# Attention's probabilities times values: from query-pair by key-pair groups to single key tiles, with the logits one to two steps ahead

## The chip, the core and the metric

The kernel runs on one core of a Trainium2 chip. The core has five engines with an instruction queue each: TensorE (PE in the profile; the loading of its weights is listed apart as PEld), VectorE (DVE), ScalarE (ACT), GpSimd (POOL) and SyncE (SP), which here only issues transfers. The engines meet through semaphores. Data lies in SBUF (128 partitions); TensorE writes to PSUM, which has eight banks of 128 x 512 float32. Sixteen DMA engines move data between HBM and SBUF.

The metric is the device time of one execution in microseconds (us), the median of several. A profiled execution gives one trace, whose span is a little shorter than that execution's own time.

## What is computed

A decoder block on one sequence of 1024 tokens and 1024 features, all in float32:

```python
xn   = rmsnorm(h, norm_mix_g);  proj = xn @ w_in
q, k, v = proj[:, :512], proj[:, 512:1024], proj[:, 1024:1536]      # 8 heads of 64
log_f = log_sigmoid(proj[:, 2560:] + b_forget);  c = cumsum(log_f)
logits = q @ k.T / 8 + c[:, None] - c[None, :], causal              # per head
att  = softmax(logits) @ v
u, vg = gelu(proj[:, 1536:2560]) in two halves                      # 8 groups of 64
sg   = u * (tril(w_spatial) @ rmsnorm(vg) per chunk of 128 + b_spatial)
h    = h + concat(att, sg) @ w_out
h    = h + (silu(g) * a) @ w_down,  a, g = causal conv3(rmsnorm(h) @ w_up)
out  = rmsnorm(h, norm_final_g)
```

TensorE takes a rounded float32 (fp32r) at full speed, so each operand is kept as a rounded high part and a low remainder, and a product is three matmuls: high x high, high x low, low x high.

## The kernel before

The whole program is one unrolled stream. The large products (`w_in`, `w_up`, `w_down`) are done by a seven-product block scheme, with sums and differences of blocks on VectorE and GpSimd. The stages in order of time: gate and value projections (from 0 us), queries and keys (from 106 us), spatial gating and the first head's logits (from about 180 us), the eight heads of attention (229 to 370 us), the output projection and second norm (from 370 us), the up products with the convolution (to 842 us), and the down products with the last norm (842 to 1058 us).

The order of an engine's instructions is set by the tile framework's scheduler from the order in which the program writes them, but for edges written by hand: `seq` chains every matmul and transpose of attention on TensorE in program order, `after` puts one instruction behind another on an engine, and while `act.on` and `dve.on` are set ScalarE and VectorE keep program order too (as they do in the first stage). A tile is a slot of a ring with a name; a new tile waits until the old one's last reader is done.

**One head of attention, before.** The queries are eight tiles of 128 rows (j = 0 to 7), the keys eight tiles of 128 (k). `logits_mm(h, j)` computes query tile j against the keys 0 to j with two matmuls for each 512 columns (L906, L907) into an "L" tile of two PSUM banks; there are two such tiles. `logits_min` (L919, VectorE) adds the causal mask, stores the row into `places[h, j//2]` in SBUF and takes the row's minimum (the logits carry a minus sign); `logits_exp` (L929, ScalarE) turns it into probabilities in place and sums the rows. `turn_p` (L935) transposes up to four 128 x 128 blocks of probabilities into one bank (L946, TensorE), ScalarE rounds them to the high part (L947), VectorE forms the low part (L948); the pair lies in a "pt" tile, of which there are three. `values` (L953) multiplies by the values: the stationary operand is V of one key tile, high and low part side by side (128 columns), the moving one the transposed probabilities.

A group was a pair of query tiles i (j = 2i and 2i + 1) by a pair of key tiles k0, k0 + 1: ten groups a head, in the order i = 3, 2, 1, 0. A matmul of a group covers one key tile and 256 query columns (128 on the diagonal). The result of four query tiles is gathered in one bank, `po`, and read by ScalarE and VectorE (L973, L974) when its last group is done.

The loop runs over 40 steps, five a head, two groups a step. In step n it issues the transposes of step n + 1, then the values of step n, and behind each group of values the logits of the next head that the table `NEXT` names: tile 7 in step 0, 6 in step 1, 5 and 4 in step 2, 3 and 2 in step 3, 1 and 0 in step 4. The exponentials of these run one step later, behind the step's casts (`last`, `due`; at the end of head 6 two batches are held back by a step). `fill` issues pieces of an independent product at the end of a step (`sg_out`: 12 matmuls of 512 columns each, the gating half of the output projection); `FILLS` names the steps: 0, 2 and 4 of head 0, and 1 and 4 of heads 1 to 5. Pieces, transposed groups and `po` share the other four banks. Heads 6 and 7 have no piece left, head 7 has no next head.

**The first tile, the gate's norm, the end.** The first stage loads x and weights in turns (L222, L223), scales x by its gain into high and low (`own`: ScalarE, then VectorE), splits the weights (`tsplit`: ScalarE high, VectorE low) and multiplies (`tmul`). `gate_norm` (L459) scales the gate's values with four wide VectorE multiplications (L466). The last stage ends with `finish` for the token tiles 4 to 7 (L1589): a square root, a reciprocal, one half of the row on ScalarE (tile 6: on VectorE, L1603), the other on VectorE (L1599), and one transfer to the output (L1604).

## Time and profile before

| what | value |
|---|---|
| median of 3 runs | 1058.76 us (1058.74 to 1059.16) |
| the profiled execution's own time, its span | 1059.72 us, 1058.0 us |
| TensorE busy | 1046.3 us (99%) |
| VectorE, ScalarE, GpSimd busy | 884.0 us (84%), 571.1 us (54%), 235.8 us (22%) |
| TensorE clock granted, mean | 0.999 |
| moved by DMA | 155.78 MB, 147 GB/s |

A row of a group view reads: line, engine, operation, output <- inputs, shapes, xcount, then busy time and mean duration of one, then the idle time of the engine before these instructions and what ended it. A row of the timeline reads: start in us, duration (of a merged run: from its start to its end), engine, line, operation, xcount, and in brackets the wait before it and what ended that. Durations of matmuls hold their latency, so that neighbours overlap: the time that one costs in a stream is the distance from start to start.

### The profile page before, as it was taken

Reading aid. Unit: us, or ns where it says so; the run is one execution under the profiler, and the core shown is the slowest. Engines: PE = TensorE matmul, PEld = TensorE weight load, DVE = VectorE, ACT = ScalarE, POOL = GpSimd, SP = SyncE. Lnnn points to the kernel's source line nnn. Section 1 sums busy time; section 2 is a strip of 40 time slices with the busy share of each in tenths; the row PEclk is TensorE's granted clock in tenths of the full one; section 3 lists DMA queues with packets and bytes.
Section 4 is the critical chain, followed back from the end, with each engine's and each line's share of the span. In section 5 each row is a group of like instructions: output and inputs, shape, how many; then the busy total and the mean of one; then the engine's idle time right before and its main releaser. Section 6 shows DMA issues by size and latency. Waiting matters only on the chain.

```text
span 1058.0 us, 14612 instructions
## 1 busy us (share of the span) xinstructions
PE 1046.3 (99%) x5156; PEld 880.3 (83%) x5156; DVE 884.0 (84%) x1297; ACT 571.1 (54%) x1013; POOL 235.8 (22%) x177
## 2 busy tenths in 40 slices
PE   9999999999999999999999999999999999999997
PEld 6988888988889888888888888888888888888885
DVE  6999787777778869998999989989897866897774
ACT  6776544456766746654444444444444544454653
POOL 0003241420420740154333323323321000000000
PEclk9999999999999999999999999999999999999999
DMA  9623466856555344222255322331322899333432
GB/s 323 219 8 134 129 162 167 224 153 190 168 163 170 122 174 173 72 89 100 80 170 179 120 96 94 120 122 59 132 96 80 302 328 314 102 99 100 146 119 94
DMA packets 67184, 155.78 MB, mean 147 GB/s; under 512 B 9028, under 2 KB 9748, under 8 KB 67112
## 3 DMA queue, kind: packets, MB, share of 16 engines
q1 hardware_dynamic: 65800, 154.82, 45.8%
q8 instruction: 40, 0.66, 0.3%
q14 instruction: 32, 0.26, 0.1%
q10 hardware_dynamic: 1312, 0.04, 0.1%
HBM read 111.96 MB, written 42.87 MB: 146 GB/s over the span
## 4 chain that ended last, share of the span: by engine, by line
PE 94%; DVE 2%; DMA 1%; ACT 1%; POOL 1%; issue 0%; SPq 0%; POOLq 0%; ACTq 0%; DVEq 0%
PE k L1529 20%; PE qc L1271 11%; PE qa L1271 11%; PE qd L1271 11%; PE ps L259 5%; PE qb L1271 5%; PE pb L259 5%; PE pb L965 3%; PE pb L946 3%; PE qa L417 2%; PE qc L417 2%; PE qd L417 2%; PE pl L906 2%; PE pl L907 2%; PE pf L990 1%; PE pf L992 1%
## 5 line engine op out<-in xcount | busy, mean ns | idle before, releaser
L1529 PE MATMUL k<-whb,wha 128*128 128x512 f32 x924 | 209.7, 389 | 0.0
L1529 PEld LDWEIGHTS k<-whb,wha 128*128 128x128 f32 x924 | 173.4, 188 | 36.2 <-DVE wha L161 0.2
L1271 PE MATMUL qc<-xT,whb 128*128 128x512 f32 x540 | 129.8, 389 | 0.2 <-ACT whb L155 0.2
L1271 PE MATMUL qa<-xB,wha 128*128 128x512 f32 x528 | 127.5, 390 | 0.0
L1271 PEld LDWEIGHTS qc<-xT,whb 128*128 128x128 f32 x540 | 101.3, 188 | 21.5 <-ACT whb L155 0.5
L1271 PEld LDWEIGHTS qa<-xB,wha 128*128 128x128 f32 x528 | 98.8, 188 | 20.9 <-DVE wha L161 0.4
L155 ACT CAST wha<-sg 128x512 fp32r<-128x512 f32 x77 | 47.8, 622 | 96.7 <-PE k L1529 86.4
L155 ACT CAST whb<-sg 128x512 fp32r<-128x512 f32 x82 | 50.5, 618 | 88.0 <-PE qc L1271 67.7
L161 DVE TENSOR_TENSOR wha<-sg,wha 128x512 fp32r<-128x512 f32 x77 | 52.7, 687 | 40.5 <-ACT wha L155 40.4
L947 ACT CAST pt<-pb 128x512 fp32r<-128x512 f32 (+1 forms) x80 | 42.2, 544 | 43.1 <-PE pb L946 34.2
L1271 PE MATMUL qd<-xB,whb 128*128 128x512 f32 x264 | 63.7, 389 | 0.0
L1271 PE MATMUL qd<-xT,whb 128*128 128x512 f32 x264 | 63.7, 389 | 0.0
L1155 POOL TENSOR_TENSOR sg<-raw 128x512 f32<-128x512 f32 x20 | 31.1, 1556 | 139.5 <-DVE whb L161 78.0
L1271 PE MATMUL qb<-xT,whb 128*128 128x512 f32 x252 | 61.0, 389 | 0.0
L161 DVE TENSOR_TENSOR whb<-sg,whb 128x512 fp32r<-128x512 f32 x82 | 57.0, 697 | 4.4 <-ACT whb L155 4.3
L948 DVE TENSOR_TENSOR pt<-pb,pt 128x512 fp32r<-128x512 f32 (+1 forms) x80 | 48.8, 634 | 12.3 <-ACT pt L947 11.0
L1271 PEld LDWEIGHTS qd<-xT,whb 128*128 128x128 f32 x264 | 49.5, 188 | 10.5 <-DVE u L1378 0.3
L1271 PEld LDWEIGHTS qd<-xB,whb 128*128 128x128 f32 x264 | 49.6, 188 | 10.3
L1271 PEld LDWEIGHTS qb<-xT,whb 128*128 128x128 f32 x252 | 47.2, 188 | 10.0 <-DVE whb L161 0.3
L965 PE MATMUL pb<-pt,V 128*128 128x256 f32 x320 | 52.1, 287 | 0.3 <-DVE pt L948 0.2
L1158 POOL TENSOR_TENSOR sg<-sg,raw 128x512 f32<-128x512 f32 x20 | 33.0, 1650 | 63.8 <-DVE whb L161 63.8
L965 PEld LDWEIGHTS pb<-pt,V 128*128 128x128 f32 x320 | 43.8, 190 | 2.6 <-DVE pt L948 0.4
(411 smaller groups left out, 2271.8 us busy)
## 6 DMA issues: line engine op xcount, KB each, us to landing
raw<-wup SPq DMA_DIRECT2D x44, 512.0 KB
sg<-hx SPq DMA_DIRECT2D x77, 256.0 KB
hx<-hs SPq DMA_DIRECT2D x44, 256.0 KB
hx<-ca SPq DMA_DIRECT2D x35, 256.0 KB
xT<-wdn SPq DMA_DIRECT2D x28, 256.0 KB
x<-kd SPq DMA_DIRECT2D x24, 256.0 KB
A<-xtok SPq DMA_DIRECT2D x8, 512.0 KB
raw<-wqk SPq DMA_DIRECT2D x8, 512.0 KB
```

Of the source, the lines that this page charges most:

```text
L155: act.copy(h, src)
L161: return eng.tensor_tensor(out=l, in0=src, in1=f32(h), op=ALU.subtract)
L259: pe.matmul(banks[m], xs(n, xi, k)[:, ms], w[:, wi, :], start=(first and k == 0 and c == 0 and (own or m % 2 == 0)), stop=(k == 3 and c == ...
L417: pe.matmul(ps, w[:, wi, ks], xs(n, xi, k), start=(first and c == 0), stop=(c == 11), skip_group_check=True)
L946: seq(pe.transpose(ptr[:, c:c + P], tj[jj][:, k * P:(k + 1) * P], ident))
L947: casts.append(act.copy(pt[:, 0, 0:w], ptr[:, 0:w]))
L948: los.append(dve.tensor_tensor(out=pt[:, 1, 0:w], in0=ptr[:, 0:w], in1=f32(pt[:, 0, 0:w]), op=ALU.subtract))
L965: seq(pe.matmul(po[0][:, oo:oo + n], lhs, pt[:, s, o:o + n], start=(k == 0 and s == 0), stop=(s == 1 and half)))
L1155: pool.tensor_tensor(out=s[0], in0=a21, in1=a22, op=ALU.add)
L1158: pool.tensor_tensor(out=s[3], in0=s[1], in1=a12, op=ALU.add)
L1271: pe.matmul(ps, w[:, wi, ks], xb[:, xi, k, :], start=(first and n == 0), stop=(n == 11), skip_group_check=True)
L1529: pe.matmul(banks[bk + m], xh[:, xi, ms], wh[:, wi, :], start=(first and p_ == 0 and n == 0), stop=(p_ == NP - 1 and n == 2), skip_group_c ...
```

## The change

Attention. A group is now a single key tile by up to four query tiles: nine groups a head, each exactly one bank of four blocks (`GROUPS`; small ones share a bank). `(1, k)` are the query tiles 4 to 7 against key tile k, `(0, k)` the tiles 0 to 3; `spans` lists the parts of a group with their columns. `turn_p` rounds all 512 columns. `values` does two matmuls a part (high and low of the probabilities), of 512, 384, 256 or 128 columns; `po` becomes two banks, one for each half of the queries, opened by `(1, 0)` and `(0, 2)` and read after `(1, 6)` and `(0, 3)`. The steps stay five a head, the last with one group. The next head's logits come two tiles a step in steps 0 to 3 and none in step 4. The piece of step 1 moves to step 2 in heads 1 to 5. The order edge on the reciprocal moves from the minimum of tile 6 to that of tile 5.

First stage. The first x tile is loaded in two halves around the first weights, scaled in halves, and the first weights' high part is made by VectorE. Gate. The four multiplications of `gate_norm` come behind the low part of the last values' weights (`gates["high"]`). End. Token tile 6 goes out in two halves.

```diff
--- before.py
+++ after.py
@@ -18,7 +18,7 @@
 NFF = 22
 WARM = 11
 
-FILLS = {(-1, j): 1 for j in (5, 3, 2)} | {(h, s): 1 for h in range(6) for s in ((0, 2, 4) if h == 0 else (1, 4))}
+FILLS = {(-1, j): 1 for j in (5, 3, 2)} | {(h, s): 1 for h in range(6) for s in ((0, 2, 4) if h == 0 else (2, 4))}
 FCFG = ("b", 4, 4)
 
 
@@ -218,7 +218,10 @@
     tmp = [[sb("pt", [P, 2, 512]) for _ in range(3)], [sb("t01", [P, 2, 512]), tj[:, 0], tj[:, 1]]]
     ua = [sb("raw", [P, 2, 512]) for _ in range(4)]
     gb = []
-    for k in range(4):
+    sp.dma_start(out=xr("x11", 0)[:, 0:256], in_=xT[0:P, 0:256])
+    sp.dma_start(out=ua[0][:, 0, :], in_=wuv[0, :, 0, :])
+    sp.dma_start(out=xr("x11", 0)[:, 256:512], in_=xT[0:P, 256:512])
+    for k in range(1, 4):
         load_x("x11", k, k, 0)
         sp.dma_start(out=ua[k][:, 0, :], in_=wuv[k, :, 0, :])
     sp.dma_start(out=cp, in_=cpk)
@@ -243,9 +246,12 @@
     vgt = [sb("G", [P, 4, 512]) for _ in range(2)]
     ut = [sb("A", [P, 4, 512]) for _ in range(2)]
 
+    newest = []
+
     def tsplit(src, gate=None, n=512, tag=None):
         w = sb(tag, [P, 2, n], F32R) if tag else ring(n=n)
         d = split_w(src, (w[:, 0], w[:, 1]))
+        newest[:] = [d]
         if gate:
             behind(d, gate)
         return w
@@ -269,9 +275,16 @@
     B = [bank() for _ in range(4)]
     S = [sbank() for _ in range(4)]
     act.on = dve.on = True
-    for k in range(4):
+    w = ring()
+    split_w(ua[0][:, 0, :], (w[:, 0], w[:, 1]), "dve")
+    for o in (slice(0, 256), slice(256, 512)):
+        h, l, src = xs("B11", 0, 0)[:, o], xs("B11", 1, 0)[:, o], xr("x11", 0)[:, o]
+        act.activation(h, src, AF.Copy, scale=gk(0))
+        dve.scalar_tensor_tensor(out=l, in0=src, scalar=gk(0), in1=f32(h), op0=ALU.mult, op1=ALU.subtract)
+    tmul(B, w, "B11", 0, True, apart=True)
+    for k in range(1, 4):
         own("B11", xr("x11", k), k, k)
-        tmul(B, tsplit(ua[k][:, 0, :]), "B11", k, True, apart=(k == 0))
+        tmul(B, tsplit(ua[k][:, 0, :]), "B11", k, True)
     for k in range(4):
         own("B21", xr("x21", k), k, 4 + k)
         tmul(S, tsplit(ua[k][:, 1, :]), "B21", k, True)
@@ -463,7 +476,7 @@
             for t in (0, 2):
                 v3 = vgt[hf][:, t:t + 2, :].rearrange("p t (g d) -> p (t g) d", d=64)
                 r = gms[:, hf * 32 + t * 8:hf * 32 + t * 8 + 16]
-                dve.tensor_tensor(out=v3, in0=v3, in1=r.unsqueeze(2).to_broadcast((P, 16, 64)), op=ALU.mult)
+                behind(dve.tensor_tensor(out=v3, in0=v3, in1=r.unsqueeze(2).to_broadcast((P, 16, 64)), op=ALU.mult), "high")
 
     gate_part(1, 0)
     gate_part(1, 2)
@@ -484,6 +497,7 @@
     W[0].sums()
     W[0].last_sum()
     values_high(3)
+    gates["high"] = newest[0]
     keep(S, 1)
     for m in range(4):
         dve.tensor_tensor(out=ut[1][:, m, :], in0=B[m], in1=ut[1][:, m, :], op=ALU.subtract)
@@ -918,7 +932,7 @@
         mn = sml.tile([P, 1], F32, tag="mn", name=nm("mn"))
         m = dve.tensor_tensor_reduce(out=places[h, i][jj], in0=ps[:, 0:n], in1=msk[:, 1024 - n:1024], scale=1.0,
                                      scalar=lim[:, 0:1], op0=ALU.add, op1=ALU.min, accum_out=mn)
-        if h and j == 6:
+        if h and j == 5:
             after(tc, m, recips[h - 1])
         if h and j == 3:
             after(tc, m, los[-1])
@@ -932,48 +946,52 @@
     def logits(h, j):
         logits_exp(h, j, logits_min(h, j, logits_mm(h, j, place())))
 
+    GROUPS = [((1, k),) for k in range(5)] + [((1, 5), (1, 7)), ((1, 6), (0, 2)), ((0, 0),), ((0, 1), (0, 3))]
+
+    def spans(g):
+
+        h, parts = g
+        c = 0
+        for half, k in parts:
+            j = max(k, 4 * half)
+            w = (4 * half + 4 - j) * P
+            yield half, k, j, c, w
+            c += w
+
     def turn_p(g):
 
-        h, i, k0 = g
-        tj = places[h, i]
         ptr = bank()
         pt = sb("pt", [P, 2, 512], F32R)
-        diag = k0 == 2 * i
-        blocks = [(k0, 0, 0), (k0, 1, 128)] + ([(k0 + 1, 1, 256)] if diag else
-                                              [(k0 + 1, 0, 256), (k0 + 1, 1, 384)])
-        w = 384 if diag else 512
-        for k, jj, c in blocks:
-            seq(pe.transpose(ptr[:, c:c + P], tj[jj][:, k * P:(k + 1) * P], ident))
-        casts.append(act.copy(pt[:, 0, 0:w], ptr[:, 0:w]))
-        los.append(dve.tensor_tensor(out=pt[:, 1, 0:w], in0=ptr[:, 0:w], in1=f32(pt[:, 0, 0:w]), op=ALU.subtract))
+        for half, k, j0, c, w in spans(g):
+            for j in range(j0, 4 * half + 4):
+                o = c + (j - j0) * P
+                seq(pe.transpose(ptr[:, o:o + P], places[g[0], j // 2][j % 2][:, k * P:(k + 1) * P], ident))
+        casts.append(act.copy(pt[:, 0, :], ptr))
+        los.append(dve.tensor_tensor(out=pt[:, 1, :], in0=ptr, in1=f32(pt[:, 0, :]), op=ALU.subtract))
         return pt
 
-    po = [None]
+    po = [None, None]
 
     def values(g, pt):
-        h, i, k0 = g
-        if i % 2 == 1 and k0 == 0:
-            po[0] = bank()
-        oc = (i % 2) * 256
-        for s in range(2):
-            for k in (k0, k0 + 1):
+        h, x = g[0], None
+        for half, k, j, c, w in spans(g):
+            new = (half, k) in ((1, 0), (0, 2))
+            if new:
+                po[half] = bank()
+            o = (j - 4 * half) * P
+            for s in range(2):
                 lhs = V[k // 2][:, k % 2, h, :, :].rearrange("p s d -> p (s d)")
-                half = k == 2 * i + 1
-                o = (k - k0) * 256
-                n = 128 if half else 256
-                oo = oc + (128 if half else 0)
-                seq(pe.matmul(po[0][:, oo:oo + n], lhs, pt[:, s, o:o + n], start=(k == 0 and s == 0),
-                              stop=(s == 1 and half)))
-        if i % 2 == 0 and k0 == 2 * i:
-            p, hh = h // 2, h % 2
-            o = slice((i // 2) * 512, (i // 2) * 512 + 512)
-            r = slice(hh * 64, hh * 64 + 64)
-            if attF[p] is None:
-                attF[p] = sb("H", [P, 2, 1024])
-            x = act.copy(attF[p][r, 0, o], po[0][64:128, :])
-            dve.tensor_tensor(out=attF[p][r, 0, o], in0=po[0][0:64, :], in1=attF[p][r, 0, o], op=ALU.add)
-            return x
-        return None
+                seq(pe.matmul(po[half][:, o:o + w], lhs, pt[:, s, c:c + w], start=(new and s == 0),
+                              stop=(s == 1 and (half, k) in ((1, 6), (0, 3))), skip_group_check=True))
+            if (half, k) in ((1, 6), (0, 3)):
+                p, hh = h // 2, h % 2
+                q = slice(half * 512, half * 512 + 512)
+                r = slice(hh * 64, hh * 64 + 64)
+                if attF[p] is None:
+                    attF[p] = sb("H", [P, 2, 1024])
+                x = act.copy(attF[p][r, 0, q], po[half][64:128, :])
+                dve.tensor_tensor(out=attF[p][r, 0, q], in0=po[half][0:64, :], in1=attF[p][r, 0, q], op=ALU.add)
+        return x
 
     def sg_out(whs):
         for hf in range(2):
@@ -1015,10 +1033,9 @@
                 pool.tensor_tensor(out=w[hf][:, 1], in0=src, in1=f32(w[hf][:, 0]), op=ALU.subtract)
             wo.append(w)
 
-    STEPS = [[(h, i, 2 * c) for i in (3, 2, 1, 0) for c in range(i + 1)] for h in range(8)]
-    STEPS = [s[n:n + 2] for s in STEPS for n in range(0, 10, 2)]
-
-    NEXT = (((7,), ()), ((6,), ()), ((5,), (4,)), ((3,), (2,)), ((1,), (0,)))
+    STEPS = [[(h, g) for g in GROUPS[n:n + 2]] for h in range(8) for n in range(0, 9, 2)]
+
+    NEXT = (((7,), (6,)), ((5,), (4,)), ((3,), (2,)), ((1,), (0,)), ((),))
 
     def fill(key):
         for _ in range(FILL.get(key, 0)):
@@ -1598,10 +1615,13 @@
             act.activation(y[tt][:, done], y[tt][:, done], AF.Copy, scale=r)
         dve.scalar_tensor_tensor(out=y[tt][:, todo], in0=y[tt][:, todo], scalar=r, in1=gfb[:, todo],
                                  op0=ALU.mult, op1=ALU.mult)
+        rows_ = out[tt * P:(tt + 1) * P, :]
         if tt == 6:
-
+            sp.dma_start(out=rows_[:, todo], in_=y[tt][:, todo])
             dve.tensor_scalar(out=y[tt][:, done], in0=y[tt][:, done], scalar1=r, scalar2=None, op0=ALU.mult)
-        sp.dma_start(out=out[tt * P:(tt + 1) * P, :], in_=y[tt])
+            sp.dma_start(out=rows_[:, done], in_=y[tt][:, done])
+        else:
+            sp.dma_start(out=rows_, in_=y[tt])
 
     def gain(tt, half):
         dve.tensor_tensor(out=y[tt][:, half], in0=y[tt][:, half], in1=gfb[:, half], op=ALU.mult)
```

## The prediction

> **What bounds the kernel now.** I read the page first, then the table by stage, then attention grouped by shape, then timelines of TensorE, VectorE and ScalarE inside one head, at the start and at the end.
>
> ```profile
> span 1058.0 us, 14612 instructions
> PE 1046.3 (99%) x5156; PEld 880.3 (83%) x5156; DVE 884.0 (84%) x1297; ACT 571.1 (54%) x1013; POOL 235.8 (22%) x177
> PE 94%; DVE 2%; DMA 1%; ACT 1%; POOL 1%; issue 0%; SPq 0%; POOLq 0%; ACTq 0%; DVEq 0%
> ...
> 229.40:347.00 117.60, 117.22 (x773) 105.07 (x772) 91.58 (x193) 79.73 (x180) 20.73 (x20) 1.00 0.58 171
> 347.00:371.00 24.00, 23.14 (x176) 21.09 (x174) 19.78 (x41) 19.01 (x45) 17.68 (x19) 1.00 0.42 139
> 371.00:1040.00 669.00, 668.83 (x2977) 552.52 (x2977) 577.94 (x752) 326.35 (x519) 144.78 (x88) 1.00 0.41 137
> ```
>
> The columns of the stage rows are stretch, length, then busy time and count of PE, PEld, DVE, ACT, POOL, then granted clock, DMA share, GB/s. TensorE is the bound nearly everywhere, at full clock. In attention's first six heads (to 347) it is busy 117.22 of 117.60 us while VectorE has 26 us and ScalarE 38 us to spare. In the last two heads, without filler, it loses some 0.9 us and the other two come within 4 to 5 us of it. After 371 it never rests until the tail, so what attention saves arrives at the end undiminished. The question is what the values' matmuls cost TensorE, and whether the new order leaves it waiting.
>
> **Part 1, the values' matmuls.** Their price is the distance from start to start.
>
> ```profile
> 836.08 2.72 PE qc L1271 x12
> ...
> 262.28 0.28 PE L906 MATMUL pl<-x 128*128 128x256 f32 x1
> 262.40 0.29 PE L907 MATMUL pl<-x,x 66*128 66x256 f32 x1
> 262.52 0.64 PE L965 MATMUL pb<-pt,V 128*128 128x256 f32 x4
> 263.00 0.40 PE L906 MATMUL pl<-x 128*128 128x512 f32 x1
> ...
> 265.72 0.34 PE L906 MATMUL pl<-x 128*128 128x384 f32 x1
> 265.89 0.34 PE L907 MATMUL pl<-x,x 66*128 66x384 f32 x1
> 266.07 1.04 PE L946 MATMUL pb<-ident,t 128*128 128x128 f32 x8
> 266.86 0.65 PE L965 MATMUL pb<-pt,V 128*128 128x256 f32 x4
> ...
> 268.45 0.28 PE L907 MATMUL pl<-x,x 66*128 66x128 f32 x1
> 268.56 0.45 PE L990 MATMUL pf<-whl,G 128*128 128x512 f32 x1
> ```
>
> 512 columns cost 2.72 / 12 = 0.227 us. 256 cost 0.12 (262.28 to 262.40 to 262.52, and four from 262.52 to 263.00). 384 cost 0.17 to 0.18; I take 0.175. 128 cost 0.11, hardly less than 256: so narrow a matmul pays for something other than its columns.
>
> ```profile
> L965 PE MATMUL pb<-pt,V 128*128 128x256 f32 x256 | 50.3, 304 | 0.3 <-DVE pt L948 0.2
> L965 PE MATMUL pb<-pt,V 128*128 128x128 f32 x64 | 14.3, 223 | 0.0
> L948 DVE TENSOR_TENSOR pt<-pb,pt 128x512 fp32r<-128x512 f32 x48 | 32.1, 687 | 9.6 <-ACT pt L947 9.2
> L948 DVE TENSOR_TENSOR pt<-pb,pt 128x384 fp32r<-128x384 f32 x32 | 17.2, 554 | 2.7 <-ACT pt L947 1.7
> L947 ACT CAST pt<-pb 128x512 fp32r<-128x512 f32 x48 | 27.2, 586 | 18.7 <-PE pb L946 14.2 <-PE pb L965 4.3
> L947 ACT CAST pt<-pb 128x384 fp32r<-128x384 f32 x32 | 15.3, 479 | 24.3 <-PE pb L946 20.0 <-PE pb L965 3.4 <-ACT t L869 0.9
> ```
>
> A head now has 256 / 8 = 32 matmuls of 256 columns and 8 of 128: 32 x 0.12 + 8 x 0.11 = 4.72 us. From the diff's spans a head gets 12 of 512 (key tiles 0 to 4 of the upper half, tile 0 of the lower), 4 of 384, 4 of 256 and 4 of 128: 12 x 0.227 + 4 x 0.175 + 4 x 0.12 + 4 x 0.11 = 4.34 us. The columns are the same (9216); 16 matmuls are gone, half of the 128-wide ones among them. Saved: 0.376 us a head, **3.01 us in eight heads**. The blocks transposed stay 36 a head. All of this lies on TensorE's path.
>
> The Trainium skill's TensorE page (TensorE: Matmul & The Clock Gate, Back-to-back issue gap) puts a warm matmul at N / 2.4 + 2.5 ns, that is 216, 109 and 56 ns for 512, 256 and 128 columns. By it a head would go from 3.94 to 3.90 us, and all heads together would save 0.3 us. The rows disagree (227, 120 and 110 ns) and go into the sum.
>
> Casts and low parts go from ten to nine a head, all 512 wide: VectorE 72 x 0.687 = 49.5 for 48 x 0.687 + 32 x 0.554 = 50.7 us, ScalarE 72 x 0.586 = 42.2 for 43.5. Behind TensorE this costs and brings nothing; in heads 6 and 7, where less covers them, at most 0.3 us.
>
> **Part 2, the order: logits two tiles a step, piece moved, edge moved.** Work on TensorE is unchanged; what may change is waiting.
>
> ```profile
> L919 DVE CUSTOM_DVE_ANT_0 H<-pl,t,lim x16: 876/1074/1286, 233.8 to 356.1; 128x1024 f32<-128x1024 f32 x4, 128x896 f32<-128x896 f32 x4, 128x768 f32<-128x768 f32 x4, 128x640 f32<-128x640 f32 x4
> ```
>
> Steps 0 and 1 now hold the four long minima, 4 x 1.074 = 4.3 us, beside four low parts (2.7): 7.0 us of VectorE. TensorE has there eight values matmuls (1.8), the logits of tiles 7 to 4 (4 and 2 + 2, then 2 + 2 and 2 + 2 matmuls: 0.91 + 0.80 + 0.69 + 0.67 = 3.1) and sixteen transposes (1.6, from 266.07 to 266.86 for eight): 6.5 us. So VectorE falls behind by about half a microsecond, unless durations overlap. Who would wait: logits tile 5 needs tile 7's "L" tile, free when its minimum is done. Laid out from a head's start, TensorE does transposes, values, logits 7, values, logits 6 (0.8 + 0.45 + 0.91 + 0.45 + 0.80 = 3.4), then transposes and values again, and wants that tile at 4.7; VectorE ends its two low parts at about 2.8 (cast 0.59 and low part 0.69 behind the transposes, the second behind a free "pt" tile) and the minimum 1.28 later, at 4.1. Carried on in the same way, with the next two low parts ahead of the next minima, tiles 4, 3 and 2 have margins of about 0.6, 0.3 and 0.4. Then step 2 brings the piece, 12 x 0.227 = 2.7 us without much for VectorE, in heads 1 to 5, and that is where it catches up. The exponentials of tiles 7 and 6 come in step 1 instead of steps 1 and 2; they are needed at step 4's transposes as before. The edge on the reciprocal has behind it only VectorE's low parts, and the rows it needs are summed a step earlier than now. Taken: 0. The bound of a gain: TensorE's waits in head 7, where late exponentials sit between ScalarE's casts, could go, because the next head's logits are now done a step sooner:
>
> ```profile
> 361.24 0.52 PE L946 MATMUL pb<-ident,H 128*128 128x128 f32 x3 [0.29 <-DVE pt L948]
> 365.62 0.66 PE L946 MATMUL pb<-ident,wy 128*128 128x128 f32 x4 [0.49 <-DVE pt L948]
> 362.96 0.73 ACT L929 ACTIVATE wy<-wy,mn 128x512 f32<-128x512 f32 x1
> ```
>
> From start to start TensorE loses more there than the brackets say: four transposes at 360.32 should end in 0.4 us and the next come at 361.24; three at 364.63 take until 365.62 where 0.3 would do; together 1.2 us. The bound of a loss: the last two heads have no piece, and the last step one group only, so that a transposed group's cast and low part (0.59 + 0.69) stand behind 0.9 us of values: a wait of 0.5 us in perhaps four places, 2 us.
>
> **Part 3, the first x tile in halves.**
>
> ```profile
> 2.66 0.43 SPq L193 DMA_DIRECT2D H<-xT  x1
> 6.23 3.25 PE L259 MATMUL pb<-wy,V 128*128 128x512 f32 x13 [0.99 <-ACT wy L51]
> 9.79 2.79 PE L259 MATMUL pb<-wy,V 128*128 128x512 f32 x11 [0.32 <-DVE wy L51]
> 7.62 0.72 ACT L51 ACTIVATE V<-H,g 128x512 fp32r<-128x512 f32 x1 [1.45 <-DMA H<-xT]
> 8.28 0.62 ACT L51 CAST wy<-raw 128x512 fp32r<-128x512 f32 x1
> 9.05 0.68 DVE L51 TENSOR_TENSOR wy<-raw,wy 128x512 fp32r<-128x512 f32 x1
> ```
>
> The first tile's matmuls begin at 6.23, when ScalarE has the weights' high part; with VectorE making it from a transfer that has half a tile less before it they should begin earlier. But TensorE stops again before 9.79: the second x tile lands at 7.62, ScalarE needs 0.72 for it and 0.62 for its weights, VectorE ends the low part at 9.73. None of this moves forward, so an earlier start only widens that gap. The extra transfer delays each later issue by one issue, 0.43 us, and the second tile with it; queued transfers hide most of that. Taken: +0.1, bounds 0 and +0.45.
>
> **Part 4, the gate's multiplications behind the weights.**
>
> ```profile
> 100.86 1.21 DVE L44 TENSOR_TENSOR G<-G,gms 128x1024 f32<-128x1024 f32 x1
> 103.48 1.70 PE L259 MATMUL pb<-whl,x 128*128 128x264 f32 x12
> 105.02 1.60 PE L259 MATMUL pb<-whl,t 128*128 128x264 f32 x12
> ```
>
> One of them (1.21 us) stands before the last weights' parts; the twelve matmuls from 103.48 take 1.54 where twelve of 264 columns need 12 x 0.12 = 1.45. At most 0.1 to win. Behind them now stand the query weights' low parts, wanted some microseconds later. Taken: 0, bounds -0.1 and +0.1.
>
> **Part 5, tile 6 out in halves.**
>
> ```profile
> 1051.91 0.75 DVE L1599 SCALAR_TENSOR_TENSOR y<-y,ssf,gfb 128x512 f32<-128x512 f32 x1
> 1053.09 1.24 SPq L1604 DMA_DIRECT2D out<-y  x2
> 1053.17 0.75 DVE L1599 SCALAR_TENSOR_TENSOR y<-y,ssf,gfb 128x512 f32<-128x512 f32 x1
> 1053.80:1056.50 2.70, 0.00 (x0) 0.00 (x0) 0.12 (x1) 0.09 (x1) 0.00 (x0) 0.81 0.96 387
> ```
>
> Tile 6 is issued at 1053.09 and tile 7 at about 1053.95; the DMA engines work at 0.96 from 1053.8 to 1056.5, so tile 7 queues behind tile 6. Half of tile 6 is ready at 1052.66, 0.43 earlier, and that much of the queue moves forward. One more issue fits on SP before 1053.95. **-0.4**, bounds 0 and -0.45.
>
> **The sum**: -3.0 + 0 + 0.1 + 0 - 0.4 = -3.3 us. The profiled execution has 1058.0 of span and 1.7 around it, 1059.72, which is 0.96 above the median of the runs; it would become 1056.4, and the median 1058.76 - 3.3 = **1055.4**.
>
> **The rivals.**
>
> A. Columns alone set the time, nothing is saved by merging: 9216 columns are the same before and after, Part 1 gives 0, 1058.5. The row of 128 columns at 0.11 speaks against it. It is also what the Trainium skill's gap rule above comes to.
>
> B. VectorE becomes the bound in steps 0 and 1: if it enters a head with some 1.1 us undone, the margins of 0.3 to 0.6 us at the "L" tiles are overrun and TensorE waits 0.8 us in each of the seven heads with logits behind them: +5.6, 1061.0, slower than before. Against it: 26 us idle in six heads and a piece before each new head. It decides from 0.45 us a head on.
>
> C. Heads 6 and 7, without pieces, wait at four places of 0.5 us for casts and low parts: +2.0, 1057.4.
>
> D. Head 7's waits go as well: -1.2 more, 1054.2, or with smaller waits elsewhere gone 1053.6.
>
> **How the numbers follow.** This kernel's measurement tells 0.2%, 2.1 us, from no change: below 1056.6 is faster, above 1060.9 slower. Forecast 0.64 (own range 1054.4 to 1056.6), A 0.05, B 0.08, C 0.10, D 0.13. Faster is the forecast, nearly all of it, and D: 0.77; the same is A, C and the forecast's upper edge: 0.15; slower is B. The range reaches down to D's 1053.6 and up to past C, 1057.6, leaving out B and most of A.
>
> **What would show it.** Values' matmuls as x96 of 512, x32 each of 384, 256 and 128, at 0.227 us in a stream; attention's stretch from 229.4 to its end about 137.5 us instead of 140.7. The first stage's second batch still starting at 9.8 to 10.2 with a longer wait before it. The output's last transfer done 0.4 us sooner after the last matmul. The forecast is wrong if idle time appears before L906 behind a minimum (B), or before L946 or L965 behind L948 in heads 6 and 7 (C).

## The result and the profile after

The changed kernel takes **1055.37 us** (median of 6 runs, 1055.21 to 1055.89) against 1058.77 us for the kernel before (6 runs beside it, 1058.4 to 1059.17): ratio 0.9967, 95% interval 0.9956 to 0.9978. The forecast was 1055.4 us, with a range of 1053.6 to 1057.6. The profiled execution took 1055.89 us, its span 1054.2.

First the page, then the table by stage (columns as in the prediction), both of the changed kernel. The stretches are cut 0.3 to 4 us earlier than before, since everything from attention on comes earlier.

```profile
span 1054.2 us, 14328 instructions
PE 1043.7 (99%) x5028; PEld 874.0 (83%) x5028; DVE 883.1 (84%) x1291; ACT 568.4 (54%) x1005; POOL 234.7 (22%) x177
...
L984 PE MATMUL pb<-pt,V 128*128 128x512 f32 (+3 forms) x192 | 49.6, 362 | 0.4 <-DVE pt L970 0.3
...
229.10:343.00 113.90, 113.64 (x675) 99.64 (x674) 90.25 (x187) 78.30 (x176) 20.05 (x20) 1.00 0.62 176
343.00:367.00 24.00, 22.89 (x145) 19.40 (x144) 19.91 (x39) 17.95 (x42) 18.17 (x19) 1.00 0.45 150
367.00:1040.00 673.00, 672.83 (x2996) 555.73 (x2995) 578.86 (x753) 327.44 (x521) 145.16 (x88) 1.00 0.41 136
```

TensorE has 128 instructions fewer (5156 to 5028), the 320 matmuls of the values having become 192, and 2.6 us less busy time. It still is the bound: 113.64 of 113.90 us in the first heads, all of the stretch behind attention, and a loss of 1.1 us in the last two heads.

Four points of the trace divide the time: the first query product (105.0 to 106.7 us in all kernels run here), the first transpose of attention, the first matmul of the output projection, and the start of the last down matmul.

| stretch, us | before | after |
|---|---|---|
| start to the first query product | 106.46 | 106.39 |
| first query product to the first transpose | 123.01 | 122.80 |
| first transpose to first output projection (attention) | 140.62 | 137.22 |
| first output projection to the last down matmul's start | 680.61 | 680.59 |
| from there to the end of the span | 7.32 | 7.17 |

Attention's 3.40 us are as much as the whole difference of the medians, and not a tenth of a us of it is given back in the 680 us behind. (The two profiled executions differ by 3.8 us; the other stretches hold the rest.) Grouped by shape, attention's matmuls of values in the changed kernel:

```profile
L984 PE MATMUL pb<-pt,V 128*128 128x512 f32 x96 | 32.3, 421 | 0.1
...
L984 PE MATMUL pb<-pt,V 128*128 128x384 f32 x32 | 9.2, 362 | 0.3 <-DVE pt L970 0.3
L984 PE MATMUL pb<-pt,V 128*128 128x256 f32 x32 | 5.7, 300 | 0.0
L984 PE MATMUL pb<-pt,V 128*128 128x128 f32 x32 | 5.3, 248 | 0.0
...
L920 PE MATMUL pl<-x 128*128 128x256 f32 x15 | 4.3, 289 | 0.0
```

The counts are the forecast's. The start, from the timelines of TensorE and ScalarE:

```profile
5.60 6.43 PE L265 MATMUL pb<-wy,V 128*128 128x512 f32 x24
...
6.85 0.72 ACT L51 ACTIVATE V<-H,g 128x512 fp32r<-128x512 f32 x1 [0.53 <-DMA H<-xT]
...
62.18 2.83 PE L265 MATMUL ps<-wy,H 128*128 128x512 f32 x11 [0.21 <-DVE wy L51]
```

The first tile's matmuls begin at 5.60 instead of 6.23, and the second tile's follow without the gap that stood before 9.79: the second x tile had landed by 6.85, not 7.62. But at 62.18 TensorE waits for weights, where before it didn't, and at the first query product 0.07 us are left. The end, from the timelines of TensorE and SP's queue and a table by stretch:

```profile
1046.54 0.84 PE L1546 MATMUL k<-whb,wha 128*128 128x512 f32 x3
...
1049.00 0.33 SPq L1620 DMA_DIRECT2D out<-y  x1
...
1049.40 0.41 SPq L1622 DMA_DIRECT2D out<-y  x1
...
1050.29 0.33 SPq L1624 DMA_DIRECT2D out<-y  x1
...
1050.10:1052.80 2.70, 0.00 (x0) 0.00 (x0) 0.13 (x1) 0.10 (x1) 0.00 (x0) 0.74 0.89 352
```

Tile 6's halves are issued 0.4 us apart, the first as soon as it is ready. The stretch shown lies as far from the last matmuls as the one of before (1053.80 to 1056.50): it moves 352 GB/s at a DMA share of 0.89, where with tile 6 in one transfer it was 387 at 0.96.

### The profile page after: what moved, and what is told of

Same layout as the page of the kernel before. It is cut to its first block, busy times and chain, and to the rows that moved or that the text cites. A ratio compares the mean times of both kernels' runs of the same rounds, so it can differ in the third digit from the quotient of the medians.

```text
span 1054.2 us, 14328 instructions
## 1 busy us (share of the span) xinstructions
PE 1043.7 (99%) x5028; PEld 874.0 (83%) x5028; DVE 883.1 (84%) x1291; ACT 568.4 (54%) x1005; POOL 234.7 (22%) x177
## 4 chain that ended last, share of the span: by engine, by line
PE 90%; DVE 4%; DMA 2%; ACT 2%; issue 1%; SPq 0%; ACTq 0%; DVEq 0%
PE k L1546 20%; PE qc L1288 11%; PE qa L1288 11%; PE qd L1288 11%; PE qb L1288 5%; PE ps L265 4%; PE pb L984 3%; PE pb L968 2%; PE pb L265 2%; PE qa L430 2%; PE qc L430 2%; PE qd L430 2%; PE pl L920 1%; PE pl L921 1%; PE pf L1008 1%; PE pf L1009 1%
## 5 line engine op out<-in xcount | busy, mean ns | idle before, releaser
L969 ACT CAST pt<-pb 128x512 fp32r<-128x512 f32 x72 | 40.5, 585 | 41.5 <-PE pb L968 36.1
L970 DVE TENSOR_TENSOR pt<-pb,pt 128x512 fp32r<-128x512 f32 x72 | 47.9, 688 | 15.1 <-ACT pt L969 14.9
L984 PE MATMUL pb<-pt,V 128*128 128x512 f32 (+3 forms) x192 | 49.6, 362 | 0.4 <-DVE pt L970 0.3
L1175 POOL TENSOR_TENSOR sg<-sg,raw 128x512 f32<-128x512 f32 x20 | 33.4, 1672 | 63.3 <-DVE whb L161 63.3
L1173 POOL TENSOR_TENSOR sg<-sg,raw 128x512 f32<-128x512 f32 x20 | 35.1, 1754 | 47.2 <-issue 44.6
```

Source lines behind the costliest of these rows:

```text
L969: casts.append(act.copy(pt[:, 0, :], ptr))
L970: los.append(dve.tensor_tensor(out=pt[:, 1, :], in0=ptr, in1=f32(pt[:, 0, :]), op=ALU.subtract))
L984: seq(pe.matmul(po[half][:, o:o + w], lhs, pt[:, s, c:c + w], start=(new and s == 0), stop=(s == 1 and (half, k) in ((1, 6), (0, 3))), ski ...
L1173: pool.tensor_tensor(out=s[1], in0=s[0], in1=a11, op=ALU.add)
L1175: pool.tensor_tensor(out=s[3], in0=s[1], in1=a12, op=ALU.add)
```

## The experiments

Twelve kernels were run. Those with the same number under "before" ran on one chip and share the runs of the kernel before.

| kernel | median us (runs) | before | ratio, 95% interval | attention us |
|---|---|---|---|---|
| e1 attention's parts alone | 1055.44 (6) | 1058.82 | 0.9968, 0.9956 to 0.9980 | 137.26 |
| e2 first x tile whole | 1054.52 (5) | 1058.82 | 0.9960, 0.9948 to 0.9973 | 137.24 |
| e3 tile 6 in one transfer | 1055.21 (5) | 1058.82 | 0.9965, 0.9952 to 0.9977 | 137.27 |
| e4 gate without the edge | 1055.60 (5) | 1058.82 | 0.9968, 0.9956 to 0.9981 | 137.25 |
| e5 values' matmuls cut to 256 columns | 1057.12 (11) | 1058.89 | 0.9983, 0.9974 to 0.9992 | 139.31 |
| e6 new groups, old order | 1066.26 (5) | 1058.89 | 1.0069, 1.0056 to 1.0081 | 148.25 |
| e7 old groups, new order | 1058.88 (11) | 1058.89 | 1.0001, 0.9992 to 1.0011 | 140.67 |
| e8 second half from ScalarE's queue | 1054.75 (5) | 1058.89 | 0.9963, 0.9951 to 0.9976 | 137.26 |
| e9 a piece moved to head 6 | 1055.59 (6) | 1058.90 | 0.9969, 0.9957 to 0.9980 | 136.85 |
| e10 the same, first x tile whole | 1055.26 (6) | 1058.90 | 0.9966, 0.9954 to 0.9978 | 136.83 |
| e11 first x tile whole, again | 1055.14 (5) | 1058.90 | 0.9963, 0.9950 to 0.9975 | 137.29 |
| e12 the change, again | 1054.96 (5) | 1058.90 | 0.9962, 0.9950 to 0.9975 | 137.22 |

The last column, read as in the table above, repeats within 0.07 us where attention's code is the same. It tells apart what medians can't.

### Each part by itself

e1 is the kernel before with attention's part of the diff alone; e2, e3 and e4 are the changed kernel with one of the other parts put back as it was.

```diff
 e2
-    sp.dma_start(out=xr("x11", 0)[:, 0:256], in_=xT[0:P, 0:256])
-    sp.dma_start(out=ua[0][:, 0, :], in_=wuv[0, :, 0, :])
-    sp.dma_start(out=xr("x11", 0)[:, 256:512], in_=xT[0:P, 256:512])
-    for k in range(1, 4):
+    for k in range(4):
...
 e3
-            sp.dma_start(out=rows_[:, todo], in_=y[tt][:, todo])
...
-            sp.dma_start(out=rows_[:, done], in_=y[tt][:, done])
-        else:
-            sp.dma_start(out=rows_, in_=y[tt])
+        sp.dma_start(out=out[tt * P:(tt + 1) * P, :], in_=y[tt])
...
 e4
-                behind(dve.tensor_tensor(out=v3, in0=v3, in1=r.unsqueeze(2).to_broadcast((P, 16, 64)), op=ALU.mult), "high")
+                dve.tensor_tensor(out=v3, in0=v3, in1=r.unsqueeze(2).to_broadcast((P, 16, 64)), op=ALU.mult)
```

> The kernel before with the attention part of the change alone (groups, order of the logits, the moved piece); first tile, gate and output as before. Theory: nearly all of the gain is here: 16 fewer matmuls a head are worth 3.0 us and the order some 0.4 more, as the changed kernel's trace suggests (last values' matmul 3.45 us nearer to attention's first transpose), so 3.0 to 3.5 us below before. Rival: a good part of the 3.4 us of the whole change comes from the first stage and the tail, then this run gains 2.5 us or less.

> The changed kernel with the first x tile loaded whole, as before. Theory: the first stage's head start of 0.5 us is lost again at about 62 us, where VectorE's low part is late behind ScalarE's waits for loads, so this run is within 0.2 us of the changed kernel. Rival 1: the head start survives in part (the changed trace has attention starting 0.28 us earlier): 0.3 us slower than the changed kernel. Rival 2: the extra transfer costs: 0.3 us faster.

> The changed kernel with token tile 6 sent out in one transfer, as before. Theory: the tail's transfers end 0.3 us later after the last matmul (5.97 us from the last matmul's start to the last packet instead of 5.65), and the time is 0.2 to 0.3 us longer than the changed kernel's. Rival: the close of the program hides it, no difference beyond 0.1 us.

> The changed kernel without the order edge on the gate's four multiplications. Theory: no difference beyond 0.1 us, since TensorE waits 0.1 us there at most. Rival: the multiplications ahead of the weights' low part cost TensorE 0.2 us or more.

e1 is 3.38 us faster than before: attention carries the result.

e4's median can't be told from the change's (1055.60 beside 1055.37), but its trace shows what the edge is for. Without it VectorE scales the gate before it makes the last weights' low part, and TensorE waits for that part:

```profile
103.80 1.61 PE L265 MATMUL pb<-whl,x 128*128 128x264 f32 x11 [0.32 <-DVE whl L44]
```

From start to start TensorE loses 0.5 us there, which is on the side of this run's rival. In before, e1 and e7, also without the edge, the stage takes only 0.07 to 0.09 us longer than in the kernels with it, as the theory had it (the lengths are given with the first x tile, below).

e3 should have been 0.2 to 0.3 us slower; its median is 0.16 us lower, so medians don't show the halves of the output. The traces do. The last packet of the output ends 5.98 us after the last down matmul's start in the four kernels that send tile 6 in one transfer (before, e1, e3, e7), and after 5.64 to 5.66 us in the ten that send halves: 0.33 us sooner. Not all of it reaches the end of the span. The span ends later than the last packet by 1.34 us in the three kernels that issue 497 transfers (before, e1, e7), by 1.41 in the four with 498 (e2, e3, e10, e11), and by 1.50 to 1.53 in the seven with 499. So each transfer more goes with about 0.1 us at the close; why, no run here shows. From the last matmul's start to the end of the span it is 7.32 and 7.06 us without and with the halves of the output where the first x tile is whole (before, e11), and 7.39 and 7.17 where it is halved (e3, e12): 0.22 to 0.26 us.

e2 came out 0.85 us faster than the change, which would speak for its second rival, an extra transfer that costs. It was run again, below.

### The number of matmuls

e5 keeps groups, order, transposes and casts of the change, and cuts each matmul of the values to at most 256 columns: 320 matmuls again, with the columns of before.

```diff
-                seq(pe.matmul(po[half][:, o:o + w], lhs, pt[:, s, c:c + w], start=(new and s == 0),
-                              stop=(s == 1 and (half, k) in ((1, 6), (0, 3))), skip_group_check=True))
+                for d in range(0, w, 256):
+                    e = min(w, d + 256)
+                    seq(pe.matmul(po[half][:, o + d:o + e], lhs, pt[:, s, c + d:c + e], start=(new and s == 0 and d == 0),
+                                  stop=(s == 1 and (half, k) in ((1, 6), (0, 3))), skip_group_check=True))
```

> The changed kernel with its values' matmuls cut into pieces of at most 256 columns: 320 of them again (256 of 256, 64 of 128), everything else as changed. Theory: it is the count that costs, 0.376 us a head, so 3.0 us slower than the changed kernel, at about 1058.4 us. Rival A: columns alone set the time, and the gain is the order's: within 0.5 us of the changed kernel.

Its values' matmuls, grouped by shape:

```profile
L986 PE MATMUL pb<-pt,V 128*128 128x256 f32 x256 | 47.3, 300 | 0.3 <-DVE pt L970 0.2
...
L986 PE MATMUL pb<-pt,V 128*128 128x128 f32 x64 | 10.8, 250 | 0.0
```

256 and 64, as in the kernel before. Attention takes 139.31 us, 2.09 more than the change and 1.31 less than before; the medians, 1.75 more and 1.77 less. So the count (of matmuls, each with its own weight load) is most of the gain, but not all, and the 3.0 us that the prediction and this run's theory gave it don't stand. The starts of each head's first transposes show where (lengths in us, from the timelines; in heads 1 to 6 all kernels have the same work between these points but for the values' matmuls):

| head | 1 | 2 | 3 | 4 | 5 | 6 | sum |
|---|---|---|---|---|---|---|---|
| before | 18.81 | 19.09 | 18.83 | 18.96 | 18.83 | 16.18 | 110.70 |
| e5 | 18.66 | 18.93 | 18.64 | 18.66 | 18.66 | 15.93 | 109.48 |
| after | 18.31 | 18.80 | 18.32 | 18.32 | 18.31 | 15.73 | 107.79 |

In heads 1, 3, 4 and 5 the change is 0.32 to 0.35 us a head faster than e5, nearly the 0.376 that 16 matmuls cost by the prediction. In heads 2 and 6 it is 0.13 and 0.20, in heads 0 and 7 it is 0.23 and 0.18. In head 2 shorter matmuls only wait longer: it takes 0.48 us more than heads 3 and 4 in the change, and 0.27 more than heads 4 and 5 in e5. Head 2 has one wait that no other head has; head 7 has the longest waits of all (both are shown with e9). By the gap that the Trainium skill (TensorE: Matmul & The Clock Gate, Back-to-back issue gap) states for an isolated matmul, the count would be worth an estimated 0.3 us in all. e5 against the change disagrees with it at 2.09.

### The groups and the order

e6 is the change with the old table of logits, the old place of the piece and of the edge; e7 is the kernel before with the new ones.

```diff
 e6
...
-    NEXT = (((7,), (6,)), ((5,), (4,)), ((3,), (2,)), ((1,), (0,)), ((),))
+    NEXT = (((7,), ()), ((6,), ()), ((5,), (4,)), ((3,), (2,)), ((1, 0),))
...
 e7
...
-    NEXT = (((7,), ()), ((6,), ()), ((5,), (4,)), ((3,), (2,)), ((1,), (0,)))
+    NEXT = (((7,), (6,)), ((5,), (4,)), ((3,), (2,)), ((1,), (0,)), ((), ()))
```

> The changed kernel with the old order of the next head's logits (7, then 6, then 5 and 4, then 3 and 2, then 1 and 0), the piece in step 1 and the edge at tile 6. Theory: the new order is worth the 0.3 us of waits that the changed trace shows less, so 0.2 to 0.6 us slower than the changed kernel, with waits again ahead of the short logits. Rival: the new groups need the early logits (all of tiles 7 to 4 before the first transpose of a head), and TensorE waits over 1 us more at the heads' boundaries: 1.5 us or more slower.

> The kernel before with the new order of logits, piece and edge, but the old groups of query pairs by key pairs, 320 matmuls. Theory: 0.3 to 0.5 us faster than before. Rival B: the long minima close together make TensorE wait at the logits' tiles: slower than before by 0.5 us or more.

e6 falls on the rival's side and beyond it: 10.9 us slower than the change, 7.4 slower than before. Its waits from 215 to 380 us (waiter, what it waited for: sum in us, times, longest), then TensorE's timeline at the end of one head, and the last exponentials on ScalarE before its wait ends:

```profile
PEld pb L968 <- ACT H L943: 6.3, 4, 1.6
...
PEld pb L968 <- ACT t L943: 5.1, 3, 1.7
PE pb L968 <- ACT H L943: 5.0, 4, 1.3
PE pb L968 <- ACT t L943: 4.1, 3, 1.4
...
306.38 0.33 PE L921 MATMUL pl<-x,x 66*128 66x384 f32 x1
308.09 1.09 PE L968 MATMUL pb<-ident,t 128*128 128x128 f32 x8 [1.38 <-ACT t L943]
...
307.13 0.81 ACT L943 ACTIVATE t<-t,mn 128x640 f32<-128x640 f32 x1
```

Once in each of seven heads the first transposes of the next head wait 1.3 to 1.4 us for exponentials, 9.1 of the 11.0 us by which attention is longer. ScalarE's row is tile 4 (640 columns). A group of the change takes key tile k from the query tiles 4 to 7 at once, so a head can't begin until the exponentials of four tiles are done; a group of before began with tiles 6 and 7. e6 takes back the order, the piece and the edge together, but what TensorE waits for is the order's. In the prediction the order was an edit worth nothing. It is what the new groups stand on.

e7 is neither faster nor slower, 0.01 us in the medians, 0.05 in attention, which is no more than attention varies. The order by itself brings nothing, and rival B of the prediction (VectorE late with the long minima at the "L" tiles) is refuted where it could be seen best, with the old groups' extra casts. But two effects hide in this nothing. In the kernel before, the logits of tile 1 waited a little for their "L" tile in heads 1 to 6, as these rows of its grouped view and its waits show:

```profile
L906 PE MATMUL pl<-x 128*128 128x256 f32 x15 | 5.0, 331 | 0.2
...
PEld pl L906 <- DVE mn L919: 0.6, 3, 0.2
```

In e7 the same row, and the transposes at a head's start:

```profile
L906 PE MATMUL pl<-x 128*128 128x256 f32 x15 | 4.6, 307 | 0.0
...
303.45 0.55 DVE L948 TENSOR_TENSOR pt<-pb,pt 128x384 fp32r<-128x384 f32 x1
...
303.49 1.29 PE L946 MATMUL pb<-ident,t 128*128 128x128 f32 x8
...
304.12 0.42 PEld L946 LDWEIGHTS pb<-ident,t 128*128 128x128 f32 x4 [0.24 <-PE pb L946]
...
304.53 1.12 PE L965 MATMUL pb<-pt,V 128*128 128x256 f32 x8
```

The wait at the logits is halved: tile 1's second matmul starts 0.22 us behind its first in the kernel before, 0.17 in e7, and 0.12, the price of 256 columns, in e5 and (but for head 6) in the change. And eight transposes take 1.04 us from start to start instead of 0.79 (266.07 to 266.86 before): 0.25 us are lost there in each head. The second four go on at 304.12, just after VectorE has ended the last low part of the head before (303.45 and 0.55 us); the bank that this frees seems to be what they wait for. In the change 289 ns stand in the row of the 256-column logits, and of waits behind a minimum its view has one left, in head 2:

```profile
PEld pl L920 <- DVE mn L933: 0.6, 1, 0.6
```

Of the 1.31 us between before and e5, 1.22 lie in heads 1 to 6 (110.70 to 109.48), 0.15 to 0.30 in each. Heads 0 and 7 together give the other 0.09; the two orders divide their work differently at the points of the table. The traces also tell on which instructions the time goes. Here are TensorE's distances from start to start, summed by the instruction at which each begins (us a head, mean of heads 1, 3, 4 and 5; one matmul of 0.03 us is left out):

| kernel | logits | values | transposes | pieces | head |
|---|---|---|---|---|---|
| before | 4.57 | 5.11 | 3.55 | 5.60 | 18.86 |
| e7 | 4.46 | 5.04 | 3.80 | 5.58 | 18.91 |
| e5 | 4.42 | 5.08 | 3.57 | 5.56 | 18.66 |
| after | 4.39 | 4.80 | 3.57 | 5.54 | 18.32 |

From before to e5 it is the wait at the logits: 0.15 of 0.20 us. In e7 the old groups give back at the transposes what the order gains elsewhere, and with the new groups (e5) the transposes don't lose it. From e5 to the change 0.28 of 0.34 us lie in the values. What the new groups would gain in the old order with 320 matmuls was not run, so that groups and order are priced together here.

### The last heads

e9 moves one piece (12 matmuls, 2.7 us) from step 0 of head 0 to step 1 of head 6, where no piece covers VectorE and ScalarE. The waits that it was to remove stand in the changed kernel's timeline of TensorE, head 7:

```profile
355.98 0.63 PE L968 MATMUL pb<-ident,H 128*128 128x128 f32 x4 [0.29 <-DVE pt L970]
...
358.07 0.66 PE L968 MATMUL pb<-ident,H 128*128 128x128 f32 x4 [0.48 <-DVE pt L970]
...
365.96 0.61 PE L984 MATMUL pb<-pt,V 128*128 128x384 f32 x3 [0.28 <-DVE pt L970]
```

```diff
-FILLS = {(-1, j): 1 for j in (5, 3, 2)} | {(h, s): 1 for h in range(6) for s in ((0, 2, 4) if h == 0 else (2, 4))}
+FILLS = {(-1, j): 1 for j in (5, 3, 2)} | {k: 1 for k in ((0, 2), (0, 4), (1, 2), (1, 4), (2, 2), (2, 4), (3, 2), (3, 4), (4, 2), (4, 4), (5, 2), (5, 4), (6, 1))}
```

> The change, with one piece of the gating product (12 matmuls of 512 columns) taken from step 0 of head 0 and put into step 1 of head 6. Theory: in heads 0 to 5 TensorE waits only because ScalarE and VectorE are a little late, in heads 6 and 7 because no piece covers them (2.7 us of waits there in the changed kernel's trace). A piece in head 6 lets VectorE and ScalarE run ahead by up to 2.7 us: attention 0.4 to 1.0 us shorter, 136.2 to 136.8 us instead of 137.2, and head 0 not longer by more than 0.2 us. Rival: the waits of head 7 come from the order inside it (no next head's logits between transposes and values), not from a backlog: nothing changes in head 7, attention within 0.2 us.

Waits of TensorE in e9, first from 340 to 368 us, then from 365 us on:

```profile
PE pb L968 <- DVE pt L970: 0.9, 2, 0.6
PE pb L984 <- DVE pt L970: 0.3, 1, 0.3
...
PE ps L1233 <- DVE xn L1215: 0.6, 1, 0.6
```

The rival is right for head 7: its waits stay. That fits the order inside it, where transposes wait for a "pt" tile behind a cast and a low part with no logits or piece between; no run took that order apart. Attention still is 0.37 us shorter, at another place: head 2's single wait of 0.45 us (18.80 becomes 18.35 us). It stood at the logits of tile 5,

```profile
274.92 0.08 DVE L933 DVE_READ_ACCUMULATOR2_ANT mn<- 128x1 f32 x1
...
275.06 0.50 PE L920 MATMUL pl<-x 128*128 128x512 f32 x1 [0.17 <-DVE mn L933]
```

behind a minimum that was late (the changed kernel's timeline); how moving the piece ends it was not followed. Nothing of it arrives: behind attention e9 takes 681.38 us to the last down matmul instead of 680.5 to 680.7, with a new wait of 0.6 us before the second norm's product (L1233). 1055.59 and 1055.26 us (e10) beside 1054.96 for the change: a wait was moved to where more stands behind it, and the 0.4 to 1.0 us that the run's theory promised didn't come.

### The first x tile

e8 issues the second half from ScalarE's queue, so that SP's has no extra issue; e10 to e12 settle e2's difference.

```diff
-    sp.dma_start(out=xr("x11", 0)[:, 256:512], in_=xT[0:P, 256:512])
+    act.dma_start(out=xr("x11", 0)[:, 256:512], in_=xT[0:P, 256:512])
```

> The changed kernel with the second half of the first x tile issued by ScalarE's queue instead of SP's. Theory: the extra issue on SP (0.47 us) sets the whole train of loads back, ScalarE waits for them in order and the head start is lost; without it attention starts some 0.3 us earlier than in the changed kernel and the time is 0.3 us shorter. Rival: the loads land when the DMA engines get to them, and the time is within 0.1 us of the changed kernel.

> The last kernel with the first x tile whole again, as in the kernel before. If the halves cost what two medians of the earlier runs suggest (0.85 us) and the piece brings 0.4 to 1.0, this is the fastest of these kernels, 1053.5 to 1054.3 us. If the first stage's differences are only the landing of its loads, it agrees with the last kernel within 0.5 us.

> The change with the first x tile whole, run again beside the change itself. Theory: the halves bring nothing that can be told from the spread of the loads' landing, the two agree within 0.5 us. Rival: the extra transfer on the first queue holds the later ones back, and this is 0.6 to 1.0 us faster than the change, as it was in the first comparison.

> The change unaltered, beside the three kernels above on the same chip: 1055.0 to 1055.8 us, attention 137.2 us from first transpose to first output projection.

Run again, the whole tile takes 1055.14 us and the halves 1054.96: the theory holds, and e2's 0.85 us did not repeat. e8 was 0.62 us below the change's first measurement (1055.37), but it is 0.21 below the second (1054.96), so its gain isn't shown. e10 lies 0.33 us from e9, which fits that the differences here are those of the loads' landing, and e12 lies 0.04 us below the times expected for it. TensorE's timelines at the start, whole (e11) and in halves (e12):

```profile
5.60 6.60 PE L262 MATMUL pb<-wy,V 128*128 128x512 f32 x24
12.04 1.29 PE L262 MATMUL pb<-whl,V 128*128 128x512 f32 x5
```

```profile
5.61 5.99 PE L265 MATMUL pb<-wy,V 128*128 128x512 f32 x24
11.43 1.75 PE L265 MATMUL pb<-whl,V 128*128 128x512 f32 x7
```

Here the whole tile starts as early as the halves, yet the third batch of matmuls starts at 12.04 with it and at 11.43 with halves. From that start to the first query product nine of the fourteen kernels take 93.97 us. The others are before, e1 and e7 (94.04 to 94.06) and e4 (94.57), which have no edge at the gate, and the changed kernel's own profile (94.52, with the wait at 62.18). So what is won in the first microseconds does arrive at the stage's end. But the third batch starts anywhere from 11.04 to 12.13 us with halves (8 kernels, 11.60 on average) and from 11.51 to 12.41 with the whole tile (6 kernels, 11.93), and the 0.33 us between the averages is less than the 0.44 between the two profiles of the change (11.87, 11.43). The first query product comes at 105.72 us on average with halves and at 105.94 with the whole tile. Whether the halves bring 0.2 to 0.3 us or nothing stays open; they don't cost 0.85, only the 0.1 us that an extra transfer adds at the close. No version ran that can be told from the change and is faster.

## Why the prediction was right

**What bounds it.** Right: from attention to the last down matmul the two kernels take the same time within 0.02 us, so each us that attention saves arrives.

**Part 1, the values' matmuls (-3.0).** Right in sign and in mechanism, and too large: the count by itself is worth 2.09 (e5). Of the 0.9 us that are missing, some 0.8 are missing in heads 0, 2, 6 and 7. In head 2 the saving turned into a longer wait behind a minimum; in the others it is likely that the same happened, but it was not followed. The text had said of heads 6 and 7 that less covers them, and then took the full saving there.

**Part 2, the order (0).** This is the term that was mis-sized. Groups and order together, without the count, are worth -1.3, by short waits of 0.15 to 0.3 us a head that the prediction had not looked for in steady heads, since a TensorE that is busy 117.22 of 117.60 us seemed to have none. Its bounds, -1.2 to +2, just miss that, and its bound of a gain came from other waits, those of head 7. The layout that found margins of 0.3 to 0.6 us at the "L" tiles holds: of the waits that the view lists, one is behind a minimum, at L920 in head 2. What the prediction did not see is that the order was no free choice: without it the new groups lose 10.9 us (e6). It said of the exponentials of tiles 7 and 6 that they are needed at step 4's transposes as before; the new groups need those of tiles 5 and 4 there as well, which it did not say.

**Part 3, the first tile (+0.1).** Its mechanism fell in the profile after: the second batch did not stay at 9.8 but came without a gap, because the second x tile landed 0.8 us earlier. In e1 and e7, whose first stage is the old one, there is no such gap either, so it came from the landing of loads in one execution. The extra transfer does cost 0.1 us, but at the close of the program and not by a later issue: that the term's size fits is luck. What the halves leave at the end of the stage is between 0 and -0.3 us, below what 14 profiles tell apart.

**Part 4, the gate (0).** Inside its bounds: the three kernels without the edge that have no other wait there (before, e1, e7) lose 0.07 to 0.09 us, and the prediction allowed 0.1. In e4 the loss was 0.6.

**Part 5, the output (-0.4).** The right direction, little more than half the size: 0.22 to 0.26 us. The first half of tile 6 does go out 0.4 us earlier, and the last packet ends 0.33 us sooner. The queue now has gaps (share 0.89 for 0.96) and tile 7 is issued no earlier than before, which fits that not all of the 0.4 arrives; another 0.1 goes to the extra transfer at the close, which the prediction had not counted.

**The sum.** That 1055.4 met 1055.37 so closely is luck. Part 1 was 0.9 us too large, Part 2 left out 1.3, and the small parts took back the rest.

**The rivals.** A: refuted by e5, where as many columns in more matmuls take 2.09 us more. B: refuted by the change and by e7; the one wait behind a minimum costs 0.45 us. C: there are waits of this kind, an estimated 2.5 us in head 7 by the distances between starts, less the price of each shape, but 2.1 were there before, so they cost 0.4 and not 2.0. D: head 7's waits did not go (0.29 and 0.48 us, beside 0.29 and 0.49 before).

Terms as measured: attention -3.40 (count -2.09, groups and order together -1.31), output -0.2 to -0.3, gate -0.1, first tile 0 to -0.3 at the stage's end and +0.1 at the close. That is 0.2 to 0.6 more than the 3.40 between the medians, of which two measurements of the change already differ by 0.4.

## What to carry to other kernels

Merging matmuls pays by what the engine spends on each above its columns, but only where the engine itself is late; in a head that waits for VectorE the saving turned into waiting, so count it head by head. An edit that looks free may be the condition of another: ask of each new grouping which inputs its first instruction needs, and when they are made. Differences below 0.5 us are better read from a stretch of the trace that repeats within 0.07 us than from medians.

## What the runs showed of the hardware

A 128-column matmul has no single price. Two of them in a row, then a transpose, in the changed kernel's timeline of TensorE:

```profile
354.89 0.22 PE L920 MATMUL pl<-x 128*128 128x128 f32 x1
354.95 0.28 PE L921 MATMUL pl<-x,x 66*128 66x128 f32 x1
355.06 0.62 PE L968 MATMUL pb<-ident,H 128*128 128x128 f32 x4
```

The second starts 0.06 us behind the first, the next instruction 0.11 behind the second: 0.085 on average, where the prediction took 0.11. The Trainium skill (TensorE: Matmul & The Clock Gate, Back-to-back issue gap) gives 81 ns as a sustained figure for 128 columns, to which this comes near, and 131 ns for 512, which the rows here don't show: they have 227.

The second is how much the start of one and the same program varies. With the first x tile whole the first matmuls began anywhere between 5.60 and 6.23 us (e11, before), in halves between 4.94 (e3) and 6.31 (e8), and the first query product came between 105.01 and 106.70. It followed the start of the third batch, by 93.97 us in nine kernels of fourteen.

The third is the close of the program: 497, 498 and 499 transfers went with 1.34, 1.41 and 1.50 to 1.53 us from the last packet to the end of the span.
